# Six buffers of split weights, moved to six different places modulo 256 bytes

## The chip, the cores and the metric

The kernel runs on one core of one Trainium2 chip, in one launch. The metric is the device time of that launch in microseconds (us). Before the change it is 1031.85 us, the median of three runs (1031.74 to 1031.96).

In this text a *place* is a byte address inside an SBUF partition modulo 256. All 128 partitions use the same addresses, so a tile has one place.

## The reference

One block of a transformer-like model on a 256 x 2048 activation, in float32:

```python
u = _rmsnorm(h, norm_mix_g)
proj = u @ w_in                       # 2048 -> 4096
u_f, q, k, v = ...                    # 1024 Fourier channels; 8 heads of 128
y_f = _fourier_mix(u_f, w_fourier)    # Re(DFT2) per group, then a 256x256 map
y_a = _dilated_attention(q, k, v)     # three (window, dilation) pairs, ALiBi
h = h + concat(y_f, y_a) @ w_out      # 2048 -> 2048
u = _rmsnorm(h, norm_mlp_g)
a = square(relu(u @ w_up))            # 2048 -> 8192
h = h + a @ w_down                    # 8192 -> 2048
return _rmsnorm(h, norm_final_g)
```

Nearly all of the work is in the products with `w_in`, `w_out`, `w_up` and `w_down`.

## The kernel before

**Three products for one.** Every float32 operand is split into a high part (`hi`, rounded to the type fp32r) and a low part (`lo`, the rest). A product is the sum of hi x hi, hi x lo and lo x hi, each an fp32r matmul on TensorE. The function `split` makes the two parts: ScalarE casts (L130), VectorE subtracts (L131).

**The weights as a list of chunks.** `_order()` lists 176 chunks, each a 128 x 2048 tile (1 MB, 8192 bytes in a partition). `load_next` loads one by DMA from the sync queue into `w_raw`, splits it into `w_hi` and `w_lo`, and runs two chunks ahead of the one in use (`AHEAD = 2`). So each of the three names has three buffers, used in turn. `chunk()` hands the next pair to TensorE.

**Two kinds of use.** The two kinds differ in which operand of the matmul is stationary (loaded into the array, 128 columns) and which is moving (streamed through).

- A *column* (`column`, L237 and L238) uses one chunk of 2048 x 128 weights as sixteen stationary tiles. The moving operand is the activation `u`, where each k-tile holds 256 columns of its high part and 256 of its low part side by side. Each k-tile takes a pair of matmuls: `w_hi` against all 512 columns, then `w_lo` against the 256 high ones. A column is 16 pairs. There are 16 columns for q and k, and 64 for `w_up`.
- A *strip* (`strip`, through `mm3`, L138 to L140) uses four chunks of 512 x 512 weights as the moving operand, 512 columns at a time. The stationary operand is the activation (`u` for `w_in`, `y_hi` and `y_lo` for `w_out` and `w_down`). A strip is 96 matmuls in the order hi x hi, hi x lo, lo x hi, so the moving operand goes `w_hi`, `w_lo`, `w_hi`.

The MLP runs in four groups (`gi` 0 to 3): 16 columns of `w_up` (256 pairs), then 4 strips of `w_down` (384 matmuls). Group 3 ends in a special form with its last output columns in pieces. The activations of groups 0 and 2 lie in one pool (`mlp`), those of groups 1 and 3 in another (`acts`).

**Side work.** Short matmuls of attention and of the Fourier part (names `aux`) are put between the chunks. In attention the product of values and probabilities (`aux<-p_hi,v_hi` and two others) has `v` as the stationary and `p` as the moving operand, and takes six matmuls of 256 columns for each head. The product of keys and queries (`aux<-kt_hi,qt_hi` and two others) has the same form.

**Where the tiles lie.** Pools are allocated one behind the other, so the place of a tile follows from the sizes of those ahead of it. Before the change `w_raw`, `w_hi`, `w_lo` (all nine buffers), `u`, and the `y` tiles in `acts` have the place 0. `v`, `kt`, `qt`, the `y` tiles in `mlp`, `g_b` and nearly all of the small tiles have the place 128; `p_hi` and `p_lo` have 64.

Of the kernel before, what the change touches and what calls it, by code (L numbers as in the profile page):

```python
# [10 lines left out]
F32 = mybir.dt.float32  # L11
F32R = mybir.dt.float32r
# [4 lines left out]
P = 128  # L17
S = 256
D = 2048
# [12 lines left out]
AHEAD = 2  # L32
FIRST = (4, 4, 2, 2, 2)
WARM = 9
FEW = 224


def _order():
# [30 lines left out]
def tile_block(ctx: ExitStack, tc: tile.TileContext, gx_t, x, w_all, w_f, g_fin,  # L69
# [2 lines left out]

    const = ctx.enter_context(tc.tile_pool(name="const", bufs=1))
    wpool = ctx.enter_context(tc.tile_pool(name="wpool", bufs=AHEAD + 1))
    acts = ctx.enter_context(tc.tile_pool(name="acts", bufs=1))
    ps_acc = ctx.enter_context(tc.tile_pool(name="ps_acc", bufs=4, space=bass.MemoryType.PSUM))
    ps_aux = ctx.enter_context(tc.tile_pool(name="ps_aux", bufs=4, space=bass.MemoryType.PSUM))
# [4 lines left out]
    def aux():  # L82
        return ps_aux.tile([P, NS], F32, name="aux")
# [7 lines left out]
    def load(out, in_):  # L91
        tc.keep_in_program_order(nc.sync.dma_start(out=out, in_=in_))  # L92
# [6 lines left out]

    few = const.tile([P, FEW], F32, name="few")  # L100
    few_at = [0]

    def small(n, *shape):
        at = few_at[0]
        few_at[0] += n
        assert few_at[0] <= FEW
        t = few[:, at:at + n]
        return t.rearrange("p (a b) -> p a b", b=shape[0]) if shape else t

    root = small(1)  # L110
    nc.scalar.activation(root, ones[:, :1], AF.Sqrt)
    busy = aux()
    for i in range(WARM):
# [13 lines left out]
    def split(hi, lo, src, scale=None):  # L127

        if scale is None:
            nc.scalar.copy(out=hi, in_=src)  # L130
            nc.vector.tensor_tensor(out=lo, in0=src, in1=f32(hi), op=ALU.subtract)  # L131
        else:
            nc.scalar.activation(hi, src, AF.Copy, scale=scale)
            nc.vector.scalar_tensor_tensor(out=lo, in0=src, scalar=scale, in1=f32(hi),
                                           op0=ALU.mult, op1=ALU.subtract)
# [11 lines left out]
    order = _order()  # L147
    loaded = []

    def load_next():  # L150
        i = len(loaded)
        raw = wpool.tile([P, D], F32, name="w_raw")
        hi = wpool.tile([P, D], F32R, name="w_hi")
        lo = wpool.tile([P, D], F32R, name="w_lo")
        cuts = FIRST[i] if i < len(FIRST) else 1
        for k in range(cuts):
            ks = slice(k * D // cuts, (k + 1) * D // cuts)
            if i < NN:
                load_x(i * CK + k * CK // cuts, CK // cuts)
            load(raw[:, ks], w_all[i, :, ks])  # L160
            if cuts > 1:
                split(hi[:, ks], lo[:, ks], raw[:, ks])
        if cuts == 1:
            for k in range(2):
                ks = slice(k * D // 2, (k + 1) * D // 2)
                split(hi[:, ks], lo[:, ks], raw[:, ks])
        _, _, nk, _, n = order[i]
        loaded.append((hi.rearrange("p (k n) -> p k n", k=nk), lo.rearrange("p (k n) -> p k n", k=nk)))

    def load_x(k0, nk):  # L170
        cols = slice(NG + k0 * S if k0 else 0, NG + (k0 + nk) * S)
        load(gh[:, cols], gx_t[:, cols])
        for k in range(k0, k0 + nk):
            split(u_hi[:, k], u_lo[:, k], xt[:, k], scale=g_cols[:, k:k + 1])
# [3 lines left out]
    def chunk():  # L178
        i = at[0]
        at[0] += 1  # L180
        while len(loaded) < min(i + 1 + AHEAD, len(order)):
            load_next()
        t = loaded[i]
        loaded[i] = None
        return t
# [507 lines left out]
```

## Time and profile before

| | |
|---|---|
| median of three runs | 1031.85 us (1031.74 to 1031.96) |
| profiled execution | 1032.38 us |
| its span, first to last instruction | 1030.6 us |
| TensorE (PE) busy, share of the span | 99% |
| VectorE (DVE), ScalarE (ACT) | 59%, 49% |
| DMA engines | 53.1%, mean 189 GB/s |
| granted TensorE clock, mean | 0.999 |

The profile counts a matmul's duration from its start to the end of its way through the array, so durations of neighbours overlap: 1280 matmuls of L237 have a mean of 396 ns but do not take 1280 times that. How fast the array goes is read from the starts: the time between the first matmul of a stage and the first of the next, divided by the number of matmuls between them.

### The profile page before, as it was taken

How to read it: one execution, taken by the hardware profiler on the slowest of the kernel's cores; microseconds unless marked ns; L12 is line 12 of the kernel's file. 1: busy time of each engine (PE TensorE's matmuls, PEld its weight loads, DVE VectorE, ACT ScalarE, POOL GpSimd, SP SyncE). 2: the span in 40 equal slices, each digit the busy share in tenths (PEclk: the TensorE clock that was granted, in tenths of full speed). 3: DMA queues.
4: the chain of work that ended last, by engine and by line, in shares of the span. 5: the costliest groups of instructions: out<-in, count | busy, mean ns of one | idle time of the engine just before them, and what ended most of it. 6: DMA issues, size and time to landing. Idle time of an engine off the chain costs nothing.

```text
span 1030.6 us, 12994 instructions
## 1 busy us (share of the span) xinstructions
PE 1021.0 (99%) x5254; PEld 868.8 (84%) x5254; DVE 609.7 (59%) x846; ACT 502.7 (49%) x741; POOL 1.3 (0%) x10
## 2 busy tenths in 40 slices
PE   9999999999999999999999999999999999999997
PEld 7888888888888888888888888888888888888886
DVE  6974875775456665544656545556554455665563
ACT  7753654554446555333555533355543335554441
POOL 0000000000000000000000000000000000000000
PEclk9999999999999999999999999999999999999999
DMA  8653745444565555455555555555545555555542
GB/s 323 229 224 118 260 168 191 162 175 163 193 217 189 180 202 189 179 204 176 193 184 184 203 180 191 203 180 188 191 179 203 177 191 197 178 197 197 180 153 82
DMA packets 32683, 195.10 MB, mean 189 GB/s; under 512 B 3568, under 2 KB 6128, under 8 KB 10608
## 3 DMA queue, kind: packets, MB, share of 16 engines
q1 hardware_dynamic: 32624, 194.28, 53.1%
q8 instruction: 41, 0.67, 0.3%
q14 instruction: 18, 0.15, 0.0%
HBM read 192.17 MB, written 2.10 MB: 188 GB/s over the span
## 4 chain that ended last, share of the span: by engine, by line
PE 97%; DMA 1%; SPq 0%; DVE 0%; ACT 0%; issue 0%; ACTq 0%
PE acc L237 29%; PE acc L139 16%; PE acc L140 16%; PE acc L138 16%; PE acc L238 15%; PE aux L138 1%; PE aux L140 1%; PE aux L139 1%; DMA w_raw<-w_all 1%; SPq L92 0%; PE aux L521 0%; PE aux L476 0%; DVE w_lo L131 0%; ACT w_hi L130 0%; ACT gh L616 0%
## 5 line engine op out<-in xcount | busy, mean ns | idle before, releaser
L131 DVE TENSOR_TENSOR w_lo<-w_raw,w_hi 128x1024 fp32r<-128x1024 f32 (+1 forms) x356 | 423.8, 1209 | 284.7 <-ACT w_hi L130 284.4
L130 ACT CAST w_hi<-w_raw 128x1024 fp32r<-128x1024 f32 (+1 forms) x356 | 362.0, 1041 | 315.4 <-PE acc L140 228.2
L237 PE MATMUL acc<-u,w_hi 128*128 128x512 f32 x1280 | 450.4, 396 | 0.0
L238 PE MATMUL acc<-u,w_lo 128*128 128x256 f32 x1280 | 359.1, 281 | 0.0
L237 PEld LDWEIGHTS acc<-u,w_hi 128*128 128x128 f32 x1280 | 240.1, 188 | 56.1
L138 PE MATMUL acc<-w_hi,y_hi 128*128 128x512 f32 x624 | 245.1, 393 | 0.0
L140 PE MATMUL acc<-w_hi,y_lo 128*128 128x512 f32 x624 | 244.4, 392 | 0.0
L139 PE MATMUL acc<-w_lo,y_hi 128*128 128x512 f32 x624 | 244.3, 391 | 0.0
L238 PEld LDWEIGHTS acc<-u,w_lo 128*128 128x128 f32 x1280 | 241.8, 189 | 0.2
L140 PEld LDWEIGHTS acc<-w_hi,y_lo 128*128 128x128 f32 x624 | 117.3, 188 | 25.8
L138 PEld LDWEIGHTS acc<-w_hi,y_hi 128*128 128x128 f32 x624 | 117.3, 188 | 25.3
L139 PEld LDWEIGHTS acc<-w_lo,y_hi 128*128 128x128 f32 x624 | 117.4, 188 | 25.1
L545 ACT ACTIVATE sq<-relu 128x256 f32<-128x256 f32 x64 | 26.7, 418 | 118.8 <-DVE relu L543 118.8
L131 DVE TENSOR_TENSOR y_lo<-sq,y_hi 128x256 fp32r<-128x256 f32 x64 | 27.2, 425 | 58.1 <-ACT y_hi L130 58.1
L139 PE MATMUL acc<-w_lo,u 128*128 128x512 f32 x120 | 47.1, 392 | 0.5 <-DVE w_lo L131 0.5
L140 PE MATMUL acc<-w_hi,u 128*128 128x512 f32 x120 | 46.8, 390 | 0.0
L138 PE MATMUL acc<-w_hi,u 128*128 128x512 f32 x120 | 46.3, 393 | 0.3 <-ACT w_hi L130 0.3
L246 DVE TENSOR_TENSOR total<-acc,total 128x256 f32<-128x256 f32 x80 | 33.5, 418 | 2.0 <-ACT total L245 1.8
L245 ACT COPY total<-acc 128x256 f32<-128x256 f32 x80 | 29.1, 364 | 6.7 <-PE acc L238 6.7
L568 DVE TENSOR_TENSOR gh<-gh,acc 128x512 f32<-128x512 f32 x30 | 20.5, 684 | 17.9 <-PE acc L140 17.9
L130 ACT CAST y_hi<-sq 128x256 fp32r<-128x256 f32 x64 | 26.0, 406 | 2.0
L543 DVE SCALAR_TENSOR_TENSOR relu<-total,inv_k 128x256 f32<-128x256 f32 x64 | 26.8, 419 | 0.0
(141 smaller groups left out, 470.3 us busy)
## 6 DMA issues: line engine op xcount, KB each, us to landing
w_raw<-w_all SPq DMA_DIRECT2D x171, 1024.0 KB, 4.8
w_raw<-w_all SPq DMA_DIRECT2D x6, 512.0 KB, 7.9
w_raw<-w_all SPq DMA_DIRECT2D x8, 256.0 KB, 4.8
gh<-x SPq DMA_DIRECT2D x8, 256.0 KB, 6.0
out<-gh SPq DMA_DIRECT2D x6, 256.0 KB, 2.4
gh<-gx_t SPq DMA_DIRECT2D x4, 256.0 KB, 6.6
wf<-w_f SPq DMA_DIRECT2D x4, 256.0 KB, 4.9
g_b<-g_fin SPq DMA_DIRECT2D x1, 1024.0 KB, 4.8
```

The lines of the kernel that those rows point to most:

```text
L130: nc.scalar.copy(out=hi, in_=src)
L131: nc.vector.tensor_tensor(out=lo, in0=src, in1=f32(hi), op=ALU.subtract)
L138: nc.tensor.matmul(ps, l_hi, r_hi, start=first, stop=False)
L139: nc.tensor.matmul(ps, l_hi, r_lo, start=False, stop=False)
L140: nc.tensor.matmul(ps, l_lo, r_hi, start=False, stop=last)
L237: nc.tensor.matmul(ps, hi[:, kt, :], r[:, kt, :], start=kt == 0, stop=False)
L238: nc.tensor.matmul(ps[:, S:], lo[:, kt, :], r[:, kt, :S], start=False, stop=kt == KT - 1)
L245: nc.scalar.copy(out=t, in_=ps[1])
L246: nc.vector.tensor_tensor(out=t, in0=ps[0], in1=t, op=ALU.add)
L543: nc.vector.scalar_tensor_tensor(out=r, in0=total(ps, mlp), scalar=0.0, in1=inv_u, op0=ALU.max, op1=ALU.mult)
L545: nc.scalar.activation(q, r, AF.Square)
L568: nc.vector.tensor_add(out=hs, in0=hs, in1=ps[m])
```

## The change

The six split buffers leave the pool `wpool` for a pool of their own, `wsplit`. Each tile is 32 or 64 bytes longer than the 8192 that it holds, so that the next one starts at the next place. A tile of 64 bytes (`first`), which nothing uses, stands ahead of them, and the tile `few` shrinks from 896 to 352 bytes.

```diff
-FEW = 224
+FEW = 88
+
+PLACES = (32, 64, 96, 160, 192, 224)
...
     wpool = ctx.enter_context(tc.tile_pool(name="wpool", bufs=AHEAD + 1))
+    wsplit = ctx.enter_context(tc.tile_pool(name="wsplit", bufs=1))
...
     root = small(1)
+    wsplit.tile([P, 16], F32, name="first")
...
+    def buffer(j):
+        room = (PLACES + (256,))[j + 1] - PLACES[j]
+        return wsplit.tile([P, D + room // 4], F32R, name=f"w_{('hi', 'lo')[j % 2]}{j // 2}")[:, :D]
+
     def load_next():
         i = len(loaded)
         raw = wpool.tile([P, D], F32, name="w_raw")
-        hi = wpool.tile([P, D], F32R, name="w_hi")
-        lo = wpool.tile([P, D], F32R, name="w_lo")
+        hi, lo = (buffer(2 * (i % (AHEAD + 1)) + j) for j in range(2))
```

The addresses that follow, in bytes of a partition:

| tile | address before | place | address after | place |
|---|---|---|---|---|
| `w_raw`, three buffers | 18432, 26624, 34816 | 0 | 17888, 26080, 34272 | 224 |
| `w_hi` of buffers 0, 1, 2 | 43008, 51200, 59392 | 0 | 42528, 58976, 75456 | 32, 96, 192 |
| `w_lo` of buffers 0, 1, 2 | 67584, 75776, 83968 | 0 | 50752, 67232, 83680 | 64, 160, 224 |
| `u` | 92160 | 0 | 91904 | 0 |
| `y_hi` in `acts` | 124928 | 0 | 124672 | 0 |
| `y_hi` in `mlp` | 186496 | 128 | 186240 | 128 |

Every tile behind the six moves down by exactly 256 bytes and keeps its place. So `w_raw` and the six are the only ones whose place changes. No instruction is added, removed or moved: on every engine the order of the instructions, their shapes and the semaphores they wait for are the same in both programs, and so are the number and size of the DMAs. In the changed kernel chunk i uses the pair of buffers i mod 3.

## The prediction

> **What bounds the kernel now.** I read the page first: the busy shares, the granted clock and the chain that ended last.
>
> ```profile
> PE 1021.0 (99%) x5254; PEld 868.8 (84%) x5254; DVE 609.7 (59%) x846; ACT 502.7 (49%) x741; POOL 1.3 (0%) x10
> PEclk9999999999999999999999999999999999999999
> PE 97%; DMA 1%; SPq 0%; DVE 0%; ACT 0%; issue 0%; ACTq 0%
> ```
>
> TensorE is the bound from end to end: 97% of the chain is PE, the clock is granted in all 40 slices, and the other engines have room. No instruction changes, so the time can only change if the same matmuls stream at another pace. So I next took the windows between the first matmuls of the MLP's eight stages (columns, strips, columns, ... of groups 0 to 3).
>
> ```profile
> core 0: us, PE busy (x) PEld busy (x) DVE busy (x) ACT busy (x) POOL busy (x), PEclk, DMA share, GB/s
> 309.91:399.88 89.97, 89.97 (x523) 79.32 (x522) 58.30 (x92) 51.88 (x85) 0.00 (x0) 1.00 0.54 187
> 399.88:489.11 89.23, 89.23 (x386) 72.35 (x385) 43.33 (x43) 33.08 (x35) 0.00 (x0) 1.00 0.54 189
> 489.11:579.55 90.44, 90.44 (x513) 78.38 (x512) 54.85 (x78) 48.38 (x77) 0.00 (x0) 1.00 0.53 187
> 579.55:666.62 87.07, 87.07 (x386) 72.11 (x385) 43.33 (x42) 33.18 (x35) 0.00 (x0) 1.00 0.54 193
> 666.62:757.06 90.44, 90.44 (x513) 78.47 (x512) 54.84 (x78) 48.40 (x77) 0.00 (x0) 1.00 0.53 187
> 757.06:846.30 89.24, 89.24 (x386) 72.36 (x385) 43.33 (x42) 33.09 (x35) 0.00 (x0) 1.00 0.54 188
> 846.30:935.05 88.75, 88.75 (x513) 78.24 (x512) 54.85 (x78) 48.42 (x77) 0.00 (x0) 1.00 0.53 190
> ```
>
> The second column is the length of a stage. Strips are 384 matmuls of 512 columns: 89.23/384 = 232.4 ns each in group 0, 87.07/384 = 226.7 in group 1, 89.24/384 = 232.4 in group 2. Clock, VectorE, ScalarE and DMA are alike in the three; what differs in the program is that `y` lies at the place 128 in groups 0 and 2 and at 0 in group 1, with the weights at 0 in all. Columns are 256 pairs: 353.3 ns a pair in groups 1 and 2, 346.7 in group 3, all with the same places (`u` 0, weights 0). So a stage settles into one of several paces, and addresses seem to have a part in which. What the chain calls PE thus hides small stalls, of about 2 to 4% of these stages.
>
> Third, the short matmuls, which have other places. I call *distance* the place of the moving minus that of the stationary operand.
>
> ```profile
> 125.67 0.28 PE L138 MATMUL aux<-p_hi,v_hi 128*128 128x256 f32 x1
> ...
> 126.35 0.39 PE L237 MATMUL acc<-u,w_hi 128*128 128x512 f32 x1
> ...
> 151.72 0.28 PE L138 MATMUL aux<-p_hi,v_hi 128*128 128x256 f32 x1
> ...
> 152.44 0.40 PE L138 MATMUL acc<-w_hi,u 128*128 128x512 f32 x1
> ...
> 135.61 0.28 PE L138 MATMUL aux<-kt_hi,qt_hi 128*128 128x256 f32 x1
> ...
> 135.97 0.39 PE L237 MATMUL acc<-u,w_hi 128*128 128x512 f32 x1
> ```
>
> These are starts of the first of a run and of what follows it. Probabilities (64) against values (128), distance -64: 0.68 us for six matmuls of 256 columns, 113.3 ns each, in the first head, and 0.72 us, 120 ns, in a head that comes after strips. Keys and queries (both 128), distance 0: 0.36 us for three, 120 ns. So at distance 0 this form runs at 120 ns, and at -64 sometimes at 113.3. The grouped durations say the same of all 16 of each kind:
>
> ```profile
> L140 PE MATMUL aux<-kt_hi,qt_lo 128*128 128x256 f32 x16 | 4.5, 282 | 0.0
> L139 PE MATMUL aux<-kt_lo,qt_hi 128*128 128x256 f32 x16 | 4.5, 282 | 0.0
> L140 PE MATMUL aux<-p_hi,v_lo 128*128 128x256 f32 x16 | 4.5, 279 | 0.0
> L139 PE MATMUL aux<-p_lo,v_hi 128*128 128x256 f32 x16 | 4.5, 279 | 0.0
> ```
>
> 282 ns at distance 0 and 279 at -64: 3 ns of the 6.7 between the two paces, so about half of the stall is gone on the average at -64.
>
> **The change part by part.** The best paces shown are 226.7 ns for 512 columns and 113.3 for 256, so 340.0 a pair. I price each part between that and the worst pace shown.
>
> *Columns.* The distance goes from 0 to the six values 256 minus 32 to 224. What is above 340.0 ns now: the four MLP stages take 89.97 + 90.44 + 90.44 + 88.75 = 359.6 us for 1024 pairs, which would be 348.2 at the best pace; of the 11.4 us over, about 1 us in group 0 belongs to ten matmuls of side work put in there (x523 for x513). The 256 pairs of attention I take at group 1's pace, 13.3 ns over (an estimate): 3.4 us. So at most 13.8 us can be gained. At the other end all columns run at 353.3: groups 0 and 3 then lose 6.7 ns on 512 pairs, 3.4 us. Nearest to the new distances are the rows at -64, where half of the stall went, so I take half: -6.9 us.
>
> *Strips with the activation at 0* (`w_in`, `w_out`, groups 1 and 3: 384 + 384 + 384 + 336 = 1488 matmuls). They run at the best pace now, so they can only lose, or stay. At distance 128 they would run at 232.4, 5.7 ns slower: 8.5 us. The new distances, 32 to 224 without 128, lie between those of the two rows, and alternate between `w_hi` and `w_lo` from one matmul to the next, for which no row stands. I take the middle, 2.85 ns: +4.2 us.
>
> *Strips with the activation at 128* (groups 0 and 2, 768 matmuls). The distance goes from 128 to the same six values. Between 0 and -4.4 us; the middle is -2.2. Nothing in the trace shows that a distance worse than 128 cannot be, so the upper ends are not hard.
>
> *The last pieces*: 96 matmuls of 256 columns with `y` and the weights at 0; half of 6.7 ns each is -0.3 us.
>
> *Loads, casts, subtractions.* DMA now writes `w_raw` at 224. The trace has a load of the same size to another place:
>
> ```profile
> w_raw<-w_all SPq DMA_DIRECT2D x171, 1024.0 KB, 4.8
> g_b<-g_fin SPq DMA_DIRECT2D x1, 1024.0 KB, 4.8
> L130 ACT CAST w_hi<-w_raw 128x1024 fp32r<-128x1024 f32 (+1 forms) x356 | 362.0, 1041 | 315.4 <-PE acc L140 228.2
> L131 DVE TENSOR_TENSOR w_lo<-w_raw,w_hi 128x512 fp32r<-128x512 f32 x8 | 5.5, 690 | 3.0 <-ACT w_hi L130 3.0
> L131 DVE TENSOR_TENSOR p_lo<-aux,p_hi 128x512 fp32r<-128x512 f32 x8 | 5.5, 686 | 0.6 <-ACT p_hi L130 0.6
> ```
>
> 4.8 us at place 128 (`g_b`) as at 0, with a chunk used in 5.5 us at the DMA share of 0.54. A subtraction takes 690 ns at place 0 and 686 at 64. ScalarE's casts mostly wait until TensorE lets a buffer go (228.2 us), so they are ahead of it. I cost this part at nothing: the cover is the two chunks loaded ahead, some 11 us. If the cover were gone, each 0.1 us that a load is late would cost up to 17 us over 171 loads, but loads would have to slow from 4.8 to over 5.5 us first. By the Trainium skill (DMA: Bandwidth & Descriptors, "How a descriptor splits into AXI transactions") a descriptor off a 256-byte boundary has one transaction more; if it held for the 8192-byte rows written here, 33 for 32 would make 4.95 us of 4.8, an estimate that stays under the cover; no run here shows it.
>
> The sum: -6.9 + 4.2 - 2.2 - 0.3 = -5.2 us against the profiled execution's 1032.38 us. The median of the runs is 0.5 us lower, 1031.85, so the forecast is 1026.7 us.
>
> **Rivals.** *The strips lose more than the columns gain.* 1488 matmuls run at their best because distance 0 lets them settle there; if alternating places keep them from settling, they run at group 0's 232.4 ns, and if the columns too only change one stalled pace for another, the time is 1031.85 + 8.5 = 1040.3 us. It decides from the point where strips at place 0 lose over (6.9 + 2.2 + 0.3)/1488 = 6.3 ns with the columns half healed, or 1.7 ns with the columns unchanged. For it speaks the head after strips, where the distance -64 did not bring the best pace; against it the first head, where it did.
>
> *All new distances are free of stalls.* Then -13.8 - 4.4 - 0.6 = -18.8: 1013 us. For it speaks that 113.3 ns row, with no stall in six matmuls; against it again the later head at 120.
>
> *Places do not matter.* The paces would then come from how a stage happened to begin, and the time stays at 1031.9, or moves by a couple of us either way. For it: the columns of groups 1 and 3 differ by 6.7 ns at the same places. Against it: groups 0 and 2 agree to 0.01 us in their strips, and differ from group 1 by 2.2 us. By the Trainium skill (TensorE: Matmul & The Clock Gate, "Step-by-step: what each phase is for") the moving operand and the loading of weights have two independent read ports, and loading "doesn't steal SBUF read bandwidth from the running matmul". By that rule the change does nothing, and the time is 1031.85 us. The trace does not agree as far as it goes: 226.7 against 232.4 ns with `y` at another place.
>
> **How the numbers follow.** Some healing of the columns that outweighs the strips: 0.40, 1026.7 us, by itself 1020 to 1030. All free: 0.10, 1013. No change, or gains and losses that cancel: 0.15, 1032. Strips lose more: 0.35, 1034 to 1041. A measurement of this kernel can tell about 0.2%, 2 us, from no change. So faster 0.50, same 0.15, slower 0.35. The bounds of the terms added up run from 1013 to 1044 (all strips at 232.4 and all columns at 353.3: 8.5 + 3.4). Leaving about one in ten at each end gives 1015 to 1040.
>
> **What would show it.** In the windows of the same eight stages: columns of about 87 to 89 us for now 88.75 to 90.44 say that the distance mattered there, and a pace that goes in threes from chunk to chunk that the buffer's place sets it. Strips of group 1 above 87.07 us are the loss, of groups 0 and 2 below 89.23 the small gain. All stages at their old lengths would mean that places do not matter. Idle time of PE before `w_raw` or the splits would make the forecast wrong in another way, and so would a distance that stalls more than 128 does.

## The result, and the profile after

The changed kernel takes 1037.67 us, the median of four runs (1037.34 to 1038.08), against 1031.82 us for the kernel before on the same chip: a ratio of 1.0057, 95% interval 1.0045 to 1.0070. It is 5.85 us slower. The forecast was 1026.7 us, faster; of the rivals, the one in which the strips lose more than the columns gain is what happened.

First the page of the changed kernel: busy shares and the chain that ended last.

```profile
span 1036.0 us, 12994 instructions
...
PE 1026.1 (99%) x5254; PEld 866.6 (84%) x5254; DVE 610.1 (59%) x846; ACT 502.3 (48%) x741; POOL 1.3 (0%) x10
...
PE 97%; DMA 1%; SPq 0%; DVE 0%; ACT 0%; issue 0%; ACTq 0%
...
w_raw<-w_all SPq DMA_DIRECT2D x171, 1024.0 KB, 4.8
```

The shape is that of before: TensorE carries 97% of the chain, with the same 5254 matmuls, and a load of a chunk still takes 4.8 us. The span grew by 5.4 us (1030.6 to 1036.0), nearly all of it in TensorE's pace: its busy time grew from 1021.0 to 1026.1. The windows of the changed kernel, from the first matmul of a stage to that of the next, show where; the first row is the four strips of `w_out`, the others are the columns and strips of the MLP's groups 0 to 3.

```profile
217.28:312.07 94.79, 94.79 (x437) 77.35 (x435) 52.48 (x64) 45.01 (x68) 0.00 (x0) 1.00 0.53 190
...
312.07:402.80 90.73, 90.73 (x523) 79.28 (x522) 58.30 (x92) 51.88 (x85) 0.00 (x0) 1.00 0.52 185
402.80:491.91 89.11, 89.11 (x387) 72.10 (x385) 43.33 (x42) 33.05 (x35) 0.00 (x0) 1.00 0.55 189
491.91:581.52 89.61, 89.61 (x513) 78.18 (x512) 54.86 (x78) 48.41 (x77) 0.00 (x0) 1.00 0.53 188
581.52:670.51 88.99, 88.99 (x386) 72.09 (x385) 43.32 (x42) 33.07 (x35) 0.00 (x0) 1.00 0.53 189
670.51:760.23 89.72, 89.72 (x514) 78.22 (x513) 54.85 (x78) 48.41 (x77) 0.00 (x0) 1.00 0.53 188
760.23:849.28 89.05, 89.05 (x386) 72.10 (x385) 43.32 (x42) 33.05 (x35) 0.00 (x0) 1.00 0.54 189
849.28:938.93 89.65, 89.65 (x514) 78.23 (x512) 54.85 (x78) 48.41 (x77) 0.00 (x0) 1.00 0.53 188
```

The strips of `w_out` before, for comparison:

```profile
216.71:309.91 93.20, 93.20 (x436) 77.38 (x435) 52.48 (x64) 45.09 (x68) 0.00 (x0) 1.00 0.56 194
```

Stage by stage against before:

| stage | before, us | after, us | difference |
|---|---|---|---|
| first three strips of `w_in` (activation at 0) | 87.35 | 88.06 | +0.7 |
| columns of attention, two stretches | 49.59, 49.44 | 49.31, 49.27 | -0.3, -0.2 |
| fourth strip of `w_in` (activation at 0) | 24.96 | 25.30 | +0.3 |
| strips of `w_out` (activation at 0) | 93.20 | 94.79 | +1.6 |
| columns, groups 0, 1, 2, 3 | 89.97, 90.44, 90.44, 88.75 | 90.73, 89.61, 89.72, 89.65 | +0.8, -0.8, -0.7, +0.9 |
| strips, groups 0 and 2 (activation at 128) | 89.23, 89.24 | 89.11, 89.05 | -0.1, -0.2 |
| strips, group 1 (activation at 0) | 87.07 | 88.99 | +1.9 |
| from the strips of group 3 (activation at 0) to the end | 95.55 | 97.07 | +1.5 |

The sum is +5.4 us. The four column stages of the MLP together move by +0.1 us and the columns of attention by -0.45, so what is lost is lost in strips with the activation at 0. In group 1 they ran at 226.7 ns a matmul and now take 88.99/384 = 231.7. The +0.7 of the first three strips is not a clear difference: among kernels whose strips all have the old distances that stage took 87.06 (`raw_alone`, below) to 87.77 us (`all_plus_32`).

Three chunks in turn in the changed kernel, columns of group 1 and then strips of group 1, for the buffers 0, 1 and 2:

```profile
514.27:519.86 5.59, 5.59 (x35) 4.90 (x33) 3.45 (x5) 3.10 (x5) 0.00 (x0) 1.00 0.53 188
519.86:525.51 5.65, 5.65 (x35) 4.89 (x34) 3.45 (x5) 3.09 (x5) 0.00 (x0) 1.00 0.55 188
525.51:531.09 5.58, 5.58 (x35) 4.89 (x34) 3.45 (x5) 3.09 (x5) 0.00 (x0) 1.00 0.53 185
598.22:603.76 5.54, 5.54 (x25) 4.51 (x24) 2.96 (x3) 2.00 (x2) 0.00 (x0) 1.00 0.51 189
603.76:609.37 5.61, 5.61 (x26) 4.50 (x25) 3.05 (x3) 2.00 (x2) 0.00 (x0) 1.00 0.53 199
609.37:614.91 5.54, 5.54 (x26) 4.51 (x25) 2.36 (x2) 2.00 (x2) 0.00 (x0) 1.00 0.54 180
```

A column is 16 pairs and a chunk of a strip 24 matmuls, so the columns run at 349, 353 and 349 ns a pair and the strips at 231, 234 and 231 ns a matmul, by buffer. The pace goes by buffer, and so by place; open is which relation of places sets it, and which part of the change costs.

### The profile page after: what moved, and what is told of

It reads as the page before. It is cut to its first block, busy times and chain, and to the rows that moved or that the text cites. A ratio compares the mean times of both kernels' runs of the same rounds, so it can differ in the third digit from the quotient of the medians.

```text
span 1036.0 us, 12994 instructions
## 1 busy us (share of the span) xinstructions
PE 1026.1 (99%) x5254; PEld 866.6 (84%) x5254; DVE 610.1 (59%) x846; ACT 502.3 (48%) x741; POOL 1.3 (0%) x10
## 4 chain that ended last, share of the span: by engine, by line
PE 97%; DMA 1%; SPq 0%; DVE 0%; ACT 0%; issue 0%; ACTq 0%
PE acc L244 29%; PE acc L143 17%; PE acc L142 16%; PE acc L144 16%; PE acc L245 15%; PE aux L142 1%; PE aux L144 1%; PE aux L143 1%; DMA w_raw<-w_all 1%; SPq L95 0%; PE aux L483 0%; PE aux L528 0%; DVE w_lo L135 0%; ACT w_hi L134 0%; ACT gh L623 0%
## 5 line engine op out<-in xcount | busy, mean ns | idle before, releaser
L143 PEld LDWEIGHTS acc<-w_lo,u 128*128 128x128 f32 x120 | 22.5, 188 | 5.6 <-DVE w_lo L135 1.0
L142 PEld LDWEIGHTS acc<-w_hi,u 128*128 128x128 f32 x120 | 22.5, 188 | 5.5 <-ACT w_hi L134 0.9
```

The costliest lines, as they stand in the source:

```text
L142: nc.tensor.matmul(ps, l_hi, r_hi, start=first, stop=False)
L143: nc.tensor.matmul(ps, l_hi, r_lo, start=False, stop=False)
```

## The experiments

Distance is, as in the prediction, the place of the moving minus that of the stationary operand, modulo 256. The theory from here on: strips run at 226.7 ns only where the distance is 0. The first rivals are that hi and lo lie at different places and the moving operand jumps between them; that `w_raw` at 224 costs; that the pool and not the place made groups 0 and 2 slow.

**`w_raw` alone** (`raw_alone`): the pool `wsplit` as in the change, but with all six places 0. The lines are against the kernel before, shortened.

```diff
-FEW = 224
+FEW = 88
+PLACES = (0, 0, 0, 0, 0, 0)
```

> The six split buffers stay at place 0 and hi and lo keep one place; only w_raw goes to 224, and all tiles behind move down by 512 bytes. Theory (distance: strips run at 226.7 ns only where the moving and the stationary operand have the same place): strips of groups 1 and 3 stay at 226.7 ns, of groups 0 and 2 at 232.4, time 1032 us within 2 us (columns may settle at 346.7 or 353.3 ns a pair). Rival (what costs is w_raw at 224, through loads or casts): strips of group 1 at about 231.7 ns and 1036 to 1038 us. Rival (alternation of places between hi and lo): as the theory here.

Measured: 1031.93 us, ratio 0.9998 (0.9988 to 1.0007). The window of the strips of group 1:

```profile
579.24:666.30 87.06, 87.06 (x386) 72.07 (x385) 43.33 (x42) 33.11 (x35) 0.00 (x0) 1.00 0.55 193
```

87.06 us for 87.07 before; every other stage of the MLP is within 0.01 us of before too. The place of the loads costs nothing that shows, within 0.1%.

**Activations of groups 0 and 2 at 0** (`y_at_0`): the kernel before with one more part on the same place.

```diff
+    mlp.tile([P, 32], F32, name="before_y")
     for gi in range(NGRP):
         hidden = [pool.tile([P, KT, S], F32R, name=f"y_{s}") for s in ("hi", "lo")]
+        if gi == 0:
+            mlp.tile([P, 32], F32, name="after_y")
```

> The kernel before, with 128 bytes put ahead of the MLP activations of groups 0 and 2 and 128 behind, so that they lie at place 0 and every other tile's place stays. Theory (distance): strips of groups 0 and 2 fall from 232.4 to 226.7 ns, 2.2 us a group, so 1027.4 us (give or take 3.4 us by the pace at which columns settle). Rival (the pool or its address range, not the place, makes groups 0 and 2 slow): still 232.4 ns, 1031.8 us.

Measured: 1029.27 us, ratio 0.9975 (0.9964 to 0.9985). Windows of the strips of group 0, the strips of group 2 and the columns of group 3:

```profile
399.50:486.58 87.08, 87.08 (x386) 72.08 (x385) 43.32 (x42) 33.19 (x35) 0.00 (x0) 1.00 0.55 193
...
754.53:841.60 87.07, 87.07 (x387) 72.08 (x385) 43.30 (x42) 33.19 (x35) 0.00 (x0) 1.00 0.55 193
841.60:932.04 90.44, 90.44 (x514) 78.48 (x512) 54.82 (x78) 48.40 (x77) 0.00 (x0) 1.00 0.53 187
```

Both groups' strips fall from 89.2 to 87.1 us, 226.7 ns. So the place, and not the pool, made them slow. The run also bears out 256 bytes as the period: the activations now start at 186624 = 729 x 256 and the weights at even multiples of 256 (43008 = 168 x 256), and an odd number of 256 bytes between them takes 87.08 us where an even one, in group 1, takes 87.07. The gain is 2.7 and not 4.4 us, because the columns of group 3, which come behind, now settle at 353.3 ns a pair (90.44 us) where they had 346.7 (88.75): at distance 0 a column stage has two paces. Its own places and instructions are the same in both kernels, so which pace it takes seems to hang on what ran ahead of it. That slow strips ahead make fast columns is no rule, though: in the kernel before, the columns of group 1 also came behind strips at 232.4 ns and ran at 353.3.

**hi and lo at one place, 32, 64, 96** (`same_32_64_96`). Here and in the next run the lines are against the changed kernel; the tile `first` and the spare bytes of each buffer follow from the places.

```diff
-FEW = 88
+FEW = 224
-PLACES = (32, 64, 96, 160, 192, 224)
+PLACES = (32, 32, 64, 64, 96, 96)
```

> hi and lo of a buffer have the same place: buffers 0, 1, 2 at 32, 64 and 96; w_raw at 0 as before. So the moving operand of a strip no longer changes its place from one matmul to the next within a chunk, but its distance to the activation is not 0. Theory (distance): strips of group 1 stay near 231 to 233 ns, as in the changed kernel, and the time is 1035 to 1039 us. Rival (alternation between hi and lo keeps strips from settling): strips of group 1 return to 227 ns, to 228 with the change of chunks, and the time is 1029 to 1033 us.

Measured, one run: 1036.93 us, where 17 runs of the kernel before beside it took 1031.3 to 1032.9. Three columns and three chunks of strips of group 1, buffers 0, 1, 2:

```profile
513.68:519.23 5.55, 5.55 (x34) 4.88 (x33) 3.45 (x5) 3.10 (x5) 0.00 (x0) 1.00 0.51 186
519.23:524.87 5.64, 5.64 (x35) 4.92 (x33) 3.46 (x5) 3.10 (x5) 0.00 (x0) 1.00 0.53 198
524.87:530.42 5.55, 5.55 (x35) 4.88 (x33) 3.45 (x5) 3.09 (x5) 0.00 (x0) 1.00 0.53 177
597.33:602.92 5.59, 5.59 (x25) 4.49 (x24) 2.96 (x3) 2.00 (x2) 0.00 (x0) 1.00 0.56 191
602.92:608.43 5.51, 5.51 (x26) 4.51 (x24) 3.05 (x3) 2.00 (x2) 0.00 (x0) 1.00 0.51 183
608.43:614.04 5.61, 5.61 (x26) 4.51 (x24) 2.36 (x2) 2.00 (x2) 0.00 (x0) 1.00 0.57 196
```

Strips at 233, 230 and 234 ns a matmul (5.59, 5.51, 5.61 us by 24): the rival of the jumping operand wanted 227 to 228 and falls. The columns show a pace for each place: 346.9, 352.5 and 346.9 ns a pair at 32, 64 and 96.

**hi and lo at one place, 128, 160, 192** (`same_128_160_192`):

```diff
-FEW = 88
+FEW = 224
-PLACES = (32, 64, 96, 160, 192, 224)
+PLACES = (128, 128, 160, 160, 192, 192)
```

> As the run with 32, 64, 96, but buffers 0, 1, 2 at 128, 160 and 192. Theory (distance): in group 1 all three chunks near 231 to 233 ns; in groups 0 and 2, where the activation lies at 128, every third chunk, that of buffer 0, at 226.7 ns and the other two at 231 to 233. Rival (alternation): all chunks of all groups at 227 to 228 ns. Rival (places do not count, only that all six are alike): 226.7 ns nowhere. Columns show the pace of distances 128, 96 and 64, one for each chunk in turn.

Measured, one run: 1037.93 us. Chunks of strips of group 0 (activation at 128), buffers 2, 0, 1, and of group 1 (activation at 0), buffers 0, 1, 2:

```profile
424.82:430.33 5.51, 5.51 (x26) 4.51 (x24) 3.05 (x3) 2.00 (x2) 0.00 (x0) 1.00 0.52 183
430.33:435.79 5.46, 5.46 (x25) 4.51 (x24) 2.36 (x2) 2.00 (x2) 0.00 (x0) 1.00 0.55 201
435.79:441.40 5.61, 5.61 (x26) 4.50 (x24) 2.36 (x2) 2.00 (x2) 0.00 (x0) 1.00 0.54 184
...
597.89:603.47 5.58, 5.58 (x26) 4.51 (x24) 2.96 (x3) 2.00 (x2) 0.00 (x0) 1.00 0.52 185
603.47:609.08 5.61, 5.61 (x26) 4.52 (x24) 3.05 (x3) 2.00 (x2) 0.00 (x0) 1.00 0.55 190
609.08:614.67 5.59, 5.59 (x26) 4.51 (x24) 2.36 (x2) 2.00 (x2) 0.00 (x0) 1.00 0.52 186
```

In group 0 the buffer at 128 has the distance 0, and of the three it alone is near the best pace: 5.46/24 = 227.5 ns with the first matmuls after the change of buffer in it. The buffer at 192 has the distance 64 there and takes 5.51 us, as the one at 64 did in group 1 of the run before. So the strip's pace goes with the distance, whichever place makes it. The table takes in three chunks of group 0 of the run before, where the buffers at 32, 64 and 96 have the distances 160, 192 and 224:

| distance | 0 | 32 | 64 | 96 | 128 | 160 | 192 | 224 |
|---|---|---|---|---|---|---|---|---|
| us for 24 matmuls | 5.46 | 5.59, 5.61 | 5.51, 5.51 | 5.61 | 5.58 | 5.61, 5.62 | 5.59, 5.60 | 5.60 |

The columns were expected to show one pace for each buffer. At 128 they do, 5.62 us; at 160 and 192 their lengths change from turn to turn at the same places: 5.64, 5.61, 5.64 us at 160 and 5.58, 5.65, 5.59 at 192, in group 1.

**All places moved by 32** (`all_plus_32`): the kernel before, with no distance of a strip or a column changed.

```diff
-FEW = 224
+FEW = 232
```

> The kernel before with every large tile 32 bytes further (a longer tile ahead of them): all places change, no distance does. Theory (distance): every stage as before, 226.7 and 232.4 ns, 1032 us within 2 us. Rival (the place itself counts, 0 is good): strips of group 1 at 230 ns or more, 1035 us or more.

Measured, one run: 1032.69 us. Strips of group 0 and of group 1:

```profile
400.19:489.42 89.23, 89.23 (x386) 72.43 (x385) 43.31 (x42) 33.10 (x35) 0.00 (x0) 1.00 0.54 190
...
579.86:666.93 87.07, 87.07 (x387) 72.13 (x385) 43.32 (x42) 33.18 (x35) 0.00 (x0) 1.00 0.56 194
```

Both as before to 0.01 us. A place by itself does not count, as far as this one shift tells.

**Other pairs of places** (`mixed_pairs`), against the changed kernel:

```diff
-PLACES = (32, 64, 96, 160, 192, 224)
+PLACES = (192, 0, 64, 0, 32, 96)
```

> Other pairs of places for hi and lo: buffer 0 at 192 and 0, buffer 1 at 64 and 0, buffer 2 at 32 and 96. It asks whether a distance of 0 in two of three matmuls (or one of three) is enough for strips to settle, and whether columns can run at 340 ns. Theory (only a distance that is 0 in every matmul settles): strips of group 1 between 229 and 234 ns in all three buffers. Rival (each matmul has the cost of its own distance): buffer 0, hi at 192 and lo at 0, (2 x 233.3 + 226.7)/3 = 231.1 ns; buffer 1, hi at 64, (2 x 228.9 + 226.7)/3 = 228.2; buffer 2 233.3. Columns: no theory has a price; 340 to 354 ns a pair.

Measured, one run: 1031.21 us. Columns and strips of group 1, buffers 0, 1, 2:

```profile
511.01:516.47 5.46, 5.46 (x34) 4.82 (x33) 3.38 (x5) 3.09 (x5) 0.00 (x0) 1.00 0.54 185
516.47:521.91 5.44, 5.44 (x34) 4.81 (x33) 3.42 (x6) 3.10 (x5) 0.00 (x0) 1.00 0.54 197
521.91:527.51 5.60, 5.60 (x34) 4.89 (x33) 3.56 (x6) 3.09 (x5) 0.00 (x0) 1.00 0.55 187
593.83:599.44 5.61, 5.61 (x25) 4.50 (x24) 2.96 (x3) 2.00 (x2) 0.00 (x0) 1.00 0.56 191
599.44:605.04 5.60, 5.60 (x26) 4.51 (x25) 3.05 (x3) 2.00 (x2) 0.00 (x0) 1.00 0.56 189
605.04:610.61 5.57, 5.57 (x25) 4.50 (x24) 2.36 (x2) 2.00 (x2) 0.00 (x0) 1.00 0.54 187
```

Strips with one matmul of three at distance 0 take 5.61 and 5.60 us, 233 to 234 ns; the rival that each matmul pays for its own distance wanted 231.1 and 228.2. So a distance that is 0 in one matmul of three does not help; 0 in two of three was not tried. In buffer 1, 64 and 0 in turn take 233.3 ns, more than either alone (229.6 and 226.7), so jumping does cost there. And the columns gave what no theory had: with hi at 64 and lo at 0 a column takes 5.44 us, 340.0 ns a pair, the best pace of the prediction's bounds; with 192 and 0 it takes 5.46, with the change from another buffer in it.

**Each use at its own place.** A buffer with some spare bytes can hold a column's chunk at one place and a strip's at another. Four kernels do so. All have `w_raw` at 224 and, where nothing else is said, the strips' chunks and all activations at 0. The lines are those of the last two; the first two do the same with one number for all six buffers.

```diff
+    def buffer(j, column):
+        t = wsplit.tile([P, D + ROOM[j] // 4], F32R, ...)
+        at = ((COLUMN[j] if column else 0) - START[j]) % 256 // 4
+        return t[:, at:at + D]
```

*Columns at 96, hi and lo alike* (`columns_96`):

> The MLP activations of groups 0 and 2 at 0 as in the earlier run, and each split buffer holds a chunk at place 0 when it is a strip's and at 96 when it is a column's (hi and lo alike); w_raw at 224. Theory (each use has a pace set by its distance): strips of all groups 226.7 ns; columns 346.6 ns a pair in all four groups, the pace of place 96 in the run with 32, 64, 96, whatever they settled at before. From 1029.3 us that is 768 pairs of groups 1 to 3 by 6.7 ns, 5.1 us less, and up to 1.7 us in attention: 1022.5 to 1024.5 us. Rival (the 346.6 ns came from how a column followed the one before it in another buffer, not from its place): columns at 353.3 in some groups, 1026 to 1030 us.

*Columns at 64* (`columns_64`), the control:

> As the run with columns at 96, but with columns at 64. Theory: columns at 353.1 ns a pair in all four groups, the pace of place 64 in the run with 32, 64, 96, and strips at 226.7: about 1030 us, group 0 slower than before by 1.7 us. Rival (settling by chance): 346.7 in some groups, 1024 to 1028 us.

Measured: 1022.71 us with columns at 96, ratio 0.9914 (0.9897 to 0.9930), and 1030.87 us with columns at 64, ratio 0.9993 (0.9983 to 1.0004). Columns of group 3, first at 96, then at 64:

```profile
836.49:925.24 88.75, 88.75 (x513) 78.11 (x512) 54.84 (x78) 48.41 (x77) 0.00 (x0) 1.00 0.55 190
```

```profile
843.06:933.50 90.44, 90.44 (x513) 78.51 (x512) 54.86 (x78) 48.40 (x77) 0.00 (x0) 1.00 0.54 186
```

That is 346.7 and 353.3 ns a pair. Groups 1 and 2 took the same as group 3 to 0.01 us, and group 0 had side work in it. The two kernels differ in nothing but these bytes, and by 8.2 us.

*The changed kernel's own columns, strips at 0* (`changed_strips_0`, `COLUMN` as the six places of the change, activations of groups 0 and 2 at 128 as before): this undoes the strips' part alone.

> The changed kernel with one part undone: a column's chunk lies at the changed kernel's six places, a strip's at 0; activations as before (groups 0 and 2 at 128). Theory (the strips at other distances than 0 are the whole loss): strips of group 1 back at 226.7 ns, of groups 0 and 2 at 232.4, columns at 348.6, 353.5 and 349.2 ns by buffer: 1037.7 less 6.2 us, 1031.5 us, 1030.5 to 1032.5. Rival (a part of the loss lies elsewhere: loads, casts, columns): above 1033 us.

Measured: 1031.86 us, ratio 1.0000 (0.9991 to 1.0009). Strips of group 1, columns of group 2 and strips of group 2:

```profile
578.48:665.55 87.07, 87.07 (x387) 72.08 (x385) 43.32 (x42) 33.10 (x35) 0.00 (x0) 1.00 0.56 194
665.55:755.26 89.71, 89.71 (x514) 78.22 (x513) 54.83 (x78) 48.42 (x77) 0.00 (x0) 1.00 0.54 188
755.26:844.86 89.60, 89.60 (x387) 72.08 (x386) 43.33 (x42) 33.06 (x35) 0.00 (x0) 1.00 0.53 187
```

Strips of group 1 are back at 87.07 us and the columns are those of the changed kernel. So the loss of 5.85 us lies in the strips with the activation at 0; the interval of the ratio leaves 0.9 us either way. One detail of the expectation was wrong: strips of group 2 took 89.60 us, 233.3 ns, not 232.4. Distance 128 too has more than one pace.

*Columns with hi at 192 and lo at 0* (`columns_192_0`), the pair found above:

> As the run with columns at 96, but a column's hi lies at 192 and its lo at 0, the pair of places that ran at 340.0 ns in one buffer of the run with mixed pairs; strips at 0 with all activations at 0. Theory (each use has the pace of its own places): 340.0 ns a pair in all four groups, 87.0 us a group for 88.8, and about 6.5 ns a pair less in attention: 1022.7 - 6.8 - 1.7 = 1014.2 us, 1013.5 to 1015.5. Rival (340.0 depends on the chunks of other buffers between): 346.7 or 353.3 in some groups, 1018 to 1030 us.

Measured: 1014.61 us, the median of five runs, ratio 0.9832 (0.9819 to 0.9845), 17.2 us faster than before. Columns and strips of group 2 and columns of group 3:

```profile
658.07:745.12 87.05, 87.05 (x513) 76.97 (x512) 54.73 (x78) 48.48 (x77) 0.00 (x0) 1.00 0.55 193
745.12:832.19 87.07, 87.07 (x387) 72.08 (x385) 43.42 (x43) 33.12 (x35) 0.00 (x0) 1.00 0.56 194
832.19:919.24 87.05, 87.05 (x513) 77.20 (x512) 54.73 (x78) 48.47 (x77) 0.00 (x0) 1.00 0.55 193
```

87.05/256 = 340.0 ns a pair and 87.07/384 = 226.7 ns a matmul, the best paces of the prediction's bounds, in one kernel. This version is faster than the kernel before and the changed one.

## Why the prediction was wrong

- *TensorE bounds, the pace is what can change, loads and casts cost nothing*: right. The order is the same, PE is busy 99%, and `w_raw` alone at 224 measured a ratio of 0.9998.
- *The columns give back half of their stalls, -6.9 us*: this is the step that failed. Measured -0.3 us: +0.1 over the four MLP stages (+0.8, -0.8, -0.7, +0.9) and -0.45 in attention. The half came from the probabilities, 256 columns in every matmul at the one distance -64 with hi and lo alike, and was applied to pairs of 512 and 256 columns at six other distances. Nor was it a property of that distance. In the kernel before, the heads do not lose half a stall each: the four that come behind columns run at 113.5 to 113.7 ns a matmul and the four behind strips at 119.5 to 119.7. In the changed kernel `p` and `v` have their old places, and yet the six matmuls of the first head, which took 0.68 us, take 0.71, 118 ns each:

```profile
126.10 0.28 PE L142 MATMUL aux<-p_hi,v_hi 128*128 128x256 f32 x1
...
126.81 0.39 PE L244 MATMUL acc<-u,w_hi 128*128 128x512 f32 x1
```

  So the row that gave the price changed with the matmuls around it. For the columns themselves, most pairs of places that were tried have one pace: 340.0 ns for hi and lo at 64 and 0, 346.7 at 96 and 96, 353.3 at 64 and 64. The six of the change are at 349, 353 and 349, about where the columns stood on the average. A possible gain of the size named was there, but at places that the change did not use.
- *Strips with the activation at 0 lose half, +4.2 us*: right in direction, too small. Measured +0.3 in the fourth strip of `w_in`, +1.6 in `w_out`, +1.9 in group 1 and +1.5 from group 3 on, 5.4 us in all, and up to 0.7 more in the first three strips, which is not clear of their scatter. Halfway between the paces of distances 0 and 128 supposes that the pace slides from one to the other. It does not: all distances tried but 0 and 64 cost about as much as 128.
- *Strips with the activation at 128 gain 2.2 us*: measured 0.3, for the same reason.
- *The last pieces gain 0.3 us*: measured 0.2. The last 72 of them start 118 ns apart where they had 120.
- *The rival that came true* was given 0.35. The time of 1037.7 us is in its range of 1034 to 1041, the strips of group 1 took 231.7 ns where it had 232.4, and the columns stayed where they were on the average, as it supposed. Its 8.5 us for the strips was too large, and its reason is not the one that the runs show: with hi and lo at one place, so that nothing alternates within a chunk, strips lose as much (230 to 234 ns in `same_32_64_96`). What spoke for it, the head after strips that ran at 120 ns at the distance -64, was the better evidence: it said that this distance has no pace of its own.
- *Places do not matter* fails: with nothing but places changed, the strips moved between 226.7 and 234 ns and the columns between 340.0 and 353.3. By the rule of the Trainium skill (TensorE: Matmul & The Clock Gate, "Step-by-step: what each phase is for") loading weights takes no read bandwidth from the running matmul, and the change would do nothing; these runs do not agree with it for fp32r operands. Why the distance counts inside the chip, no run here shows.

## What to carry to other kernels

When TensorE is busy 99% and no instruction is left to remove, divide the length of each stage by its matmuls, and compare stages that do the same work: a difference of 2 to 4% between twins was, here, a stall that could be had. Take the pace of each use from a run that has that use, with its own shapes and sequence, before pricing a change of addresses; then give each use its own place, which costs some spare bytes. Strips were best with moving and stationary operand at equal places modulo 256, and columns of 512 and 256 in turn with the 512's weights at 192 and the 256's at 0 and the moving operand at 0 (64 and 0 did as well, in the chunks of one buffer).

## What the runs showed of the hardware that was not expected

- The relation of two addresses modulo 256 moves the pace of fp32r matmuls by up to 3% (strips 226.7 to 234 ns) and 4% (pairs 340.0 to 353.3 ns), while moving all large tiles together by 32 bytes moves none of the MLP's first seven stages by more than 0.01 us.
- A stream of matmuls can keep one of several paces for a whole stage at the same addresses: columns at distance 0 at 346.7 or 353.3 ns a pair, strips at distance 128 at 232.4 or 233.3 ns. What ran ahead has a part in it: when the strips of group 2 got faster, the columns of group 3 fell to the slower pace and took back 1.7 us. By what rule, these runs do not show.
- With hi at 192 and lo at 0 the columns showed no second pace in the one trace of that kernel: 87.05 us in groups 1, 2 and 3 alike.
